# One decoder layer on one core: the first group's squares move to ScalarE and TensorE, and 1/rms comes from one reciprocal-square-root function

## The chip, the core and the metric

The kernel runs on one core of a Trainium2 chip. The core has five engines with a queue of instructions each: PE (TensorE, matmuls), DVE (VectorE), ACT (ScalarE), POOL (GpSimd) and SP (SyncE, which issues nearly all DMAs here). Each engine works through its queue in order and waits on semaphores of the others. The metric is the device time of one execution in microseconds (us).

## The reference

A layer of a hybrid decoder for 2048 prompt tokens and 8 sample tokens, model width 1024, all in float32:

```
def rms_norm(x, w):
    xf = xf * lax.rsqrt(jnp.mean(xf * xf, axis=-1, keepdims=True) + EPS)
    return (xf * w)

h = rms_norm(x, norm1_w)
q, k, v, z, xbc, dt_raw = split(h @ w_in)
a = sliding-window attention(q, k, v)              # window 128, learned sinks, relative bias
s = SSD mixer(z, xbc, dt_raw)                      # conv, scan, gate; then per group of 256 columns:
    yg = yg * lax.rsqrt(jnp.mean(yg * yg, axis=-1, keepdims=True) + EPS)
x = x + concat(a, s) @ w_out
h2 = rms_norm(x, norm2_w)
x = x + (silu(h2 @ w_gate) * (h2 @ w_up)) @ w_down
y = rms_norm(x, final_norm_w)
```

So there are four kinds of reciprocal root mean square: before the input projection, inside the SSD mixer (two per token), before the feed-forward part, and at the end.

## The kernel before, in words

Features lie on the partitions, tokens along the free axis. The 16 blocks of 128 prompt tokens are worked off in six groups: four of 384 tokens, one of 256 tokens and the 8 sample tokens (264 columns), one of 256. A float32 product is made of three fp32r matmuls (`mm3`: high times high, high times low, low times high), so each projection of one 128-column unit is 24 matmuls into one PSUM bank. A weight unit comes in two halves (`weight`, L208 to L216): SP loads the raw half, ACT makes the high part (L209), DVE the low part (L210); for a third of the units the pair is written back to HBM and read from there later (L205).

Stages are Python generators: I or X (load x, squares, 1/rms, scale), A (the dt and x/B/C projections with the convolution), K (keys, values), B (queries and gate z), P (attention), Q (SSD, then the mixer's norm), S (pair of high and low parts of the mixed heads), O (output projection), H (second norm), F (feed-forward), Z (final norm and store). The driver interleaves them by ratios written out by hand (for instance `run(("A", 0), ([("I", 0)], RI), units=UA)`); after that the tile framework's scheduler sorts the instructions of each engine by its own model of their durations, so that a small edit moves many instructions by a few places. PSUM has 8 banks, four with the tag "d" (tiles `psd`, for projections) and four with the tag "m" (tiles `psm`, for everything else).

The first group is special (`stage_x0`, kinds "I"). To let PE begin before the norm is known, x is only scaled with the norm's weight and split (L299 on ACT, L300 on DVE), and the projections run on that. What comes out of PSUM is multiplied by 1/rms afterwards (tile `r`): the dt projection in `got_dt` (L365), the x/B/C projections in `got` (L402), the keys, values, queries and z in `take`. Up to then a "d" bank stays taken. DVE squares the eight tiles of x in place (L303, eight instructions) and adds them up (L305, seven), then `rinv_b` makes 1/rms.

`rinv_b` gets the sum of squares, adds it over the partitions by one float32 matmul with a matrix of ones (`psm` from `cst`), and then has on ACT: Ln of mean plus epsilon (L695), a Copy that makes -0.5 times the mean (L697), Exp of -0.5 times the logarithm (L698), and on DVE one Newton step in three instructions (L701, L702, L703). Ln lies in another table of ACT's functions than Exp and Tanh, so an ACT_TABLE_LOAD stands ahead of the Ln and another ahead of the Exp. `rinv_b` runs for X, H and Z of every group with one sum, and for Q with two sums at once.

Tanh is used for the convolution's SiLU (L390), for z (L520) and for the feed-forward gate (L1018); Exp for softplus (L252), the SSD decays (L722, L723, L732, L749) and the softmax (L590, L592). Square, Copy and Identity never have a table load ahead of them.

Of the kernel before, what the change touches and what calls it, by code (L numbers as in the profile page):

```python
# [13 lines left out]
AF = mybir.ActivationFunctionType  # L14
ALU = mybir.AluOpType
# [14 lines left out]
DM = 1024  # L30
KT = DM // P
# [41 lines left out]
def hymba(ctx: ExitStack, tc: tile.TileContext, I: dict, O: dict, groups):  # L73
# [14 lines left out]
    def T(shape, dtype=F32, tag=None, bufs=1):  # L88
        cnt[0] += 1
        nm = f"{tag}_{cnt[0]}"  # L90
        return sb.tile(shape, dtype, tag=tag, name=nm, bufs=bufs)

    def PS(tag):
        cnt[0] += 1
        return pp.tile([P, 512], F32, tag=tag, name=f"ps{tag}_{cnt[0]}", bufs=4)
# [5 lines left out]
    V, S, G, PE, SP = nc.vector, nc.scalar, nc.gpsimd, nc.tensor, nc.sync  # L101

    def mm(o, l, r, start=True, stop=True):
        PE.matmul(o, l, r, start=start, stop=stop)  # L104
# [5 lines left out]
    ones = cst[:, C_ONE:C_ONE + P]  # L110
# [6 lines left out]
    epsc = T([P, 1], tag="epsc")  # L117
# [14 lines left out]
    bias = T([P, NH, 2 * P], tag="bias")  # L132
# [107 lines left out]
    def act_pair(home):  # L240
        return tuple(T([P, KT, NMAX], F32R, tag=home + part) for part in ("hi", "lo"))
# [27 lines left out]
    def stage_x(g):  # L269
        N, off = g["N"], g["off"]  # L270
        x = g["x"] = act_pair("a")
        xr = T([P, KT, NMAX], tag="xr")
        for h in range(2):
            ks = slice(4 * h, 4 * h + 4)
            SP.dma_start(xr[:, ks, :N], I["xT"][:, ks, off:off + N])
            yield
        sq = T([P, NMAX], tag="sq")
        yield from squares(xr, sq, N)
        yield from rinv_b(sq, N, DM)
        yield from scaled(xr, S_N1, sq, N, x, lambda m: xr[:, m, :N])  # L280


    def stage_x0(g):
        N, off = g["N"], g["off"]
        x = g["x"] = act_pair("b")
        xr = T([P, KT, NMAX], tag="xr")
        for h in range(4):
            ks = slice(2 * h, 2 * h + 2)
            SP.dma_start(xr[:, ks, :N], I["xT"][:, ks, off:off + N])
            if h == 0:  # L290
                SP.dma_start(wdr, I["wdt"])
        S.dma_start(cst, I["consts"][:, 0:C_MAIN])
        S.activation(wdt[:, :, 0:NH], wdr, AF.Copy)
        V.tensor_tensor(wdt[:, :, NH:], wdr, wdt[:, :, 0:NH].bitcast(F32), ALU.subtract)

        home = g["home"] = T([P, 2 * (FC + 1) * NMAX], tag="hc")
        r = g["r"] = T([P, NMAX], tag="m2", bufs=M2)[:, :N]
        for m in range(KT):
            S.activation(x[0][:, m, :N], xr[:, m, :N], AF.Copy, scale=col(S_N1, m))  # L299
            V.scalar_tensor_tensor(x[1][:, m, :N], xr[:, m, :N], col(S_N1, m), x[0][:, m, :N].bitcast(F32), ALU.mult, ALU.subtract)  # L300
        yield
        for m in range(KT):
            V.tensor_tensor(xr[:, m, :N], xr[:, m, :N], xr[:, m, :N], ALU.mult)  # L303
            if m:
                V.tensor_tensor(xr[:, 0, :N] if m < KT - 1 else r, xr[:, 0, :N], xr[:, m, :N], ALU.add)  # L305
            if m % 4 == 3:
                yield
        yield from rinv_b(r, N, DM)

    def take(g, ps):  # L310

# [344 lines left out]
    def stage_q(g):  # L656
        nb, N = g["nb"], g["N"]
        xbc = g["xbc"]
        for b in range(nb):
            yield from ssd(g, b)  # L660
        if g["smp"]:
            while not g.get("sdone"):
                yield
        if g["b0"] + nb == NB:
            tail_outputs(g)
        ss = []
        for q in range(2):
            s0 = T([P, NMAX], tag="tmp", bufs=6)
            s1 = T([P, NMAX], tag="tmp", bufs=6)
            S.activation(s0[:, :N], xbc[:, 2 * q, :N], AF.Square)  # L670
            S.activation(s1[:, :N], xbc[:, 2 * q + 1, :N], AF.Square)
            ss.append((s0, s1))
            yield
        for s0, s1 in ss:
            V.tensor_tensor(s0[:, :N], s0[:, :N], s1[:, :N], ALU.add)
        yield
        yield from rinv_b([s0 for s0, _ in ss], N, 256)
        for t in range(4):
            y = xbc[:, t, :N]
            V.scalar_tensor_tensor(y, y, nwc(t), ss[t // 2][0][:, :N], ALU.mult, ALU.mult)  # L680
            if t % 2:
                yield
        g["done"] = g.get("done", 0) + 1

    def rinv_b(ss, N, d):

        ss = [s[:, :N] for s in (ss if isinstance(ss, list) else [ss])]
        ps = []
        for s in ss:
            ps.append(PS("m"))  # L690
            mm(ps[-1][:, :N], ones, s)
        yield
        v = [T([P, NMAX], tag="tmp", bufs=6)[:, :N] for _ in ss]
        for s, p in zip(ss, ps):
            S.activation(s, p[:, :N], AF.Ln, bias=epsc[:, 0:1], scale=1.0 / d)  # L695
        for s, u, p in zip(ss, v, ps):
            S.activation(u, p[:, :N], AF.Copy, bias=-0.5 * EPS, scale=-0.5 / d)  # L697
            S.activation(s, s, AF.Exp, scale=-0.5)  # L698
        yield
        for s, u in zip(ss, v):  # L700
            V.tensor_tensor(u, u, s, ALU.mult)  # L701
            V.tensor_tensor(u, u, s, ALU.mult)  # L702
            V.scalar_tensor_tensor(s, u, 1.5, s, ALU.add, ALU.mult)  # L703
        yield
# [346 lines left out]
    for nb, smp in groups:  # L1051
# [6 lines left out]
    assert b0 == NB  # L1058
    n = len(gs)
    kinds = {"I": stage_x0, "X": stage_x, "A": stage_a, "K": stage_k, "B": stage_b, "P": stage_p, "Q": stage_q, "Y": stage_y,  # L1060
             "S": stage_s, "O": stage_o, "H": stage_h, "F": stage_f, "Z": stage_z}
    made = {}
# [7 lines left out]
    def run(main, *rest, units=None, drain=99):  # L1070


        rest = [e if isinstance(e, list) else [list(e[0]), e[1], 0.0] for e in rest]

        def advance(e, k):
            e[2] += k
            while e[2] >= 1 and e[0]:
                if step(*e[0][0]) == 0:
                    e[0].pop(0)
                e[2] -= 1  # L1080

        while units is None or units > 0:
            says = step(*main) if main else 0
            if says in (0, "tail"):
                break
            tick()
            for e in rest:
                advance(e, e[1])
            if units is not None:
                units -= 1  # L1090
        while any(e[0] for e in rest[:drain]):
            for e in rest[:drain]:
                e[2] = 0.0
                advance(e, 1)
            tick()
        return rest[drain:]

    def mixers(i, u):

        g = gs[i]  # L1100
        r = [([("P", i)], (g["nb"] * 20 + 1) / u), ([("Q", i)], (g["nb"] * 9 + 17 + (60 if g["smp"] else 0)) / u)]
        return r + ([([("Y", i)], 55 / (0.8 * u))] if g["smp"] else [])
# [6 lines left out]
    r = run(("A", 0), ([("X", 1)], RX1), drain=0)  # L1109
    r = run(("K", 0), *r, drain=0)  # L1110
    load_bias(bscr)
    r = run(("B", 0), *r, units=UQ, drain=0)
    r = run(("B", 0), *r, *mixers(0, U0), drain=1)
    r = run(("A", 1), *r, drain=0)
    run(("B", 1), *r, ([("S", 0)], 2), units=UB)
    run(("O", 0))
    r = run(("B", 1), ([("H", 0)], RH0), drain=0)
    run(("K", 1), *r)
    for i in range(n):
# [4 lines left out]
        elif i + 2 < n:  # L1124
            run(("F", i), *mixers(i + 1, RM), ([("X", i + 2)], RX))
            run(("F", i))
            r = run(("K", i + 2), ([("S", i + 1)], RS), ([("Z", i)], RZ), drain=0)
# [99 lines left out]
```

## Time and profile before

| what | us |
|---|---|
| median of 3 runs | 2350.46 (2349.97 to 2353.34) |
| profiled execution, its own time | 2353.68 |
| its span in the trace | 2351.9 |
| granted TensorE clock, mean over the span | 0.989 of full speed |
| DMA engines' busy share, mean rate | 75.1% on the one large queue, 252 GB/s |

The span runs from the first to the last instruction; the execution's own time is 1.8 us longer. Names in the profile are the program's tiles: `bhi,blo` and `ahi,alo` are the high and low parts of an activation pair, `w` a weight pair, `wraw` a raw weight half, `hc` the hidden tiles of the feed-forward part, `xr` the raw x, `cst` the constants with the matrix of ones, `sq`, `tmp` or `m` the tile with the sum of squares or 1/rms. `PE psd L104` is a projection's matmul (all matmuls are issued from line 104). Where a row of the timeline ends in brackets, they hold the engine's idle time before it and what ended it.

### The profile page before, as it was taken

The page shows a single profiled execution, that of the slowest core. Times are in us where ns is not written, and L with a number is a line of the kernel's source. Part 1 is how long each engine was busy: PE and PEld are TensorE (multiplying, and loading weights), DVE is VectorE, ACT ScalarE, POOL GpSimd, SP SyncE. Part 2 cuts the span into 40 slices and gives each one's busy share as a digit, 9 for nine tenths or more (in the row PEclk, how much of TensorE's full clock was granted, in tenths as well). Part 3 has the DMA queues.
Part 4 walks back from the last instruction along what each step waited for, and adds up shares of the span by engine and source line. Part 5 has one row for each costly group of instructions (what it writes and reads, how often), then busy time and mean ns, then how long its engine had stood idle before and what let it go on. Part 6 is the DMA issues. An engine that isn't in the chain of part 4 may idle for free.

```text
span 2351.9 us, 39896 instructions
## 1 busy us (share of the span) xinstructions
PE 2276.6 (97%) x14633; PEld 2224.5 (95%) x14633; DVE 1478.2 (63%) x3325; ACT 988.1 (42%) x2139; POOL 31.5 (1%) x109
## 2 busy tenths in 40 slices
PE   7995999999999999999999999999999999999997
PEld 6995999999999999999999998999999899999997
DVE  7886687866647786653566555554734567656544
ACT  5666554744444364343325333321321354434233
POOL 1000000000000000000000000000000000000000
PEclk9997999999999999999999999999999999999999
DMA  8653565666877677788777879878887987788886
GB/s 295 238 185 103 183 219 183 214 198 220 316 283 236 214 235 242 240 304 280 266 258 274 280 267 341 292 226 264 299 247 240 344 289 246 255 276 271 275 279 196
DMA packets 227230, 592.30 MB, mean 252 GB/s; under 512 B 24323, under 2 KB 64060, under 8 KB 226892
## 3 DMA queue, kind: packets, MB, share of 16 engines
q1 hardware_dynamic: 226892, 589.56, 75.1%
q8 instruction: 116, 1.90, 0.3%
q14 instruction: 78, 0.64, 0.1%
q10 hardware_dynamic: 144, 0.20, 0.0%
HBM read 479.97 MB, written 110.21 MB: 251 GB/s over the span
## 4 chain that ended last, share of the span: by engine, by line
PE 87%; DMA 6%; DVE 3%; ACT 2%; issue 1%; SPq 0%; ACTq 0%; DVEq 0%
PE psd L104 81%; PE psm L104 5%; DMA w<-wi 1%; DMA w<-wd 1%; DMA w<-wo 1%; PE psm L610 1%; DMA xr<-in_xT_dram 0%; DMA m<-sbcd 0%; DMA w<-wg 0%; DMA m<-in_sssm_dram 0%; DMA w<-wu 0%; DVE x L1045 0%; DMA big<-csd 0%; DMA out_yT_dram<-x 0%; DVE w L210 0%
## 5 line engine op out<-in xcount | busy, mean ns | idle before, releaser
L104 PE MATMUL psd<-bhi,w 128*128 128x384 f32 (+1 forms) x4448 | 1106.0, 329 | 12.6 <-DVE tmp L365 7.7
L104 PEld LDWEIGHTS psd<-bhi,w 128*128 128x128 f32 x4448 | 787.2, 189 | 20.6 <-issue 9.7
L104 PE MATMUL psd<-blo,w 128*128 128x384 f32 (+1 forms) x2224 | 727.0, 327 | 1.0 <-DVE blo L341 1.0
L209 ACT ACTIVATE w<-wraw 128x512 fp32r<-128x512 f32 (+1 forms) x543 | 324.5, 601 | 546.7 <-PE psd L104 426.4
L104 PE MATMUL psd<-hc,w 128*128 128x384 f32 (+2 forms) x3168 | 514.4, 320 | 6.2 <-DMA w<-wd 4.7
L104 PEld LDWEIGHTS psd<-hc,w 128*128 128x128 f32 x3168 | 494.4, 188 | 11.9 <-DVE sq L323 5.3
L104 PE MATMUL psd<-ahi,w 128*128 128x256 f32 (+2 forms) x2272 | 487.6, 305 | 18.4 <-DMA w<-wi 8.7
L210 DVE TENSOR_TENSOR w<-wraw,w 128x512 fp32r<-128x512 f32 (+1 forms) x543 | 353.2, 653 | 125.6 <-ACT w L209 115.8
L104 PEld LDWEIGHTS psd<-blo,w 128*128 128x128 f32 x2224 | 419.8, 189 | 2.5 <-DVE blo L341 1.3
L104 PEld LDWEIGHTS psd<-ahi,w 128*128 128x128 f32 x2272 | 377.0, 189 | 25.5 <-DMA w<-wi 7.6
L104 PE MATMUL psd<-alo,w 128*128 128x256 f32 (+2 forms) x1136 | 345.9, 305 | 0.0
L997 DVE TENSOR_TENSOR x<-psd,x 128x384 f32<-128x384 f32 (+2 forms) x336 | 169.3, 511 | 98.3 <-PE psd L104 97.6
L104 PEld LDWEIGHTS psd<-alo,w 128*128 128x128 f32 x1136 | 214.6, 189 | 1.2
L1018 ACT ACTIVATE tmp<-psd 128x384 f32<-128x384 f32 (+2 forms) x132 | 59.9, 454 | 263.0 <-PE psd L104 262.9
L1004 DVE SCALAR_TENSOR_TENSOR tmp<-tmp,psd 128x384 f32<-128x384 f32 (+2 forms) x132 | 67.0, 508 | 161.6 <-ACT tmp L1018 161.2
L1007 DVE SCALAR_TENSOR_TENSOR tmp<-psd,tmp 128x384 f32<-128x384 f32 (+2 forms) x132 | 67.7, 513 | 127.7 <-PE psd L104 127.4
L1008 ACT ACTIVATE hc<-tmp 128x384 fp32r<-128x384 f32 (+2 forms) x132 | 64.0, 485 | 142.8 <-DVE tmp L1007 142.1
L384 DVE SCALAR_TENSOR_TENSOR x<-tmp,cols,x 128x384 f32<-128x384 f32 (+1 forms) x144 | 80.6, 569 | 35.5 <-ACT x L406 26.2
L320 ACT ACTIVATE tmp<-x 128x384 f32<-128x384 f32 (+2 forms) x84 | 40.4, 487 | 102.7 <-DVE x L944 69.6
L1012 DVE TENSOR_TENSOR hc<-tmp,hc 128x384 fp32r<-128x384 f32 (+2 forms) x132 | 67.3, 510 | 16.0 <-ACT hc L1008 15.5
L323 DVE TENSOR_TENSOR sq<-sq,tmp 128x384 f32<-128x384 f32 (+2 forms) x119 | 60.5, 508 | 25.0 <-ACT tmp L320 24.1
L944 DVE TENSOR_TENSOR x<-psd,x 128x384 f32<-128x384 f32 (+2 forms) x48 | 24.7, 515 | 70.6 <-PE psd L104 70.4
(259 smaller groups left out, 1765.7 us busy)
## 6 DMA issues: line engine op xcount, KB each, us to landing
w<-wi SPq DMA_DIRECT2D x144, 512.0 KB, 5.4
w<-wu SPq DMA_DIRECT2D x133, 512.0 KB, 4.5
w<-wg SPq DMA_DIRECT2D x131, 512.0 KB, 4.6
w<-wd SPq DMA_DIRECT2D x144, 384.0 KB, 3.6
wraw<-in_wg_dram SPq DMA_DIRECT2D x133, 256.0 KB, 3.6
wraw<-in_wu_dram SPq DMA_DIRECT2D x131, 256.0 KB, 3.9
w<-wo SPq DMA_DIRECT2D x57, 512.0 KB, 4.8
wraw<-in_wd_dram SPq DMA_DIRECT2D x144, 192.0 KB, 3.6
```

What stands on the lines that cost most here:

```text
L104: PE.matmul(o, l, r, start=start, stop=stop)
L209: S.activation(hi, raw, AF.Copy)
L210: V.tensor_tensor(lo, raw, hi.bitcast(F32), ALU.subtract)
L320: S.activation(t[:, :N], x[:, m, :N], AF.Square)
L323: e.tensor_tensor(sq[:, :N], sq[:, :N], t[:, :N], ALU.add)
L384: V.scalar_tensor_tensor(acc, raw[:, j:j + NP], cwc(j, t), acc, ALU.mult, ALU.add)
L997: V.tensor_tensor(x1[:, m, :N], p[:, :N], x1[:, m, :N], ALU.add)
L1004: V.scalar_tensor_tensor(t[:, :N], t[:, :N], 1.0, pg[:, :N], ALU.add, ALU.mult)
L1007: V.scalar_tensor_tensor(t[:, :N], pu[:, :N], 0.5, t[:, :N], ALU.mult, ALU.mult)
L1008: S.activation(hh[:, 0, :N], t[:, :N], AF.Copy)
L1012: e.tensor_tensor(hl[:, 0, :N], t[:, :N], hh[:, 0, :N].bitcast(F32), ALU.subtract)
L1018: S.activation(t[:, :N], pg[:, :N], AF.Tanh, scale=0.5)
```

## The change

In `stage_x0` the squares go from DVE to ACT, and the sums from DVE to PE: each squared tile is multiplied by the matrix of ones and accumulated in one PSUM bank over eight matmuls, in place of one matmul on the finished sum. In `rinv_b`, for all groups and stages, Ln, and the Exp after it, become one function, Abs_reciprocal_sqrt; the Copy and the Newton step stay. The squares are at L304 now, the function at L697, the Copy at L699, the Newton step at L702 to L704; every line behind `rinv_b` is one higher (the feed-forward Tanh is at L1019, the first SSD Exp at L723).

```
         yield
+        ps = PS("m")
         for m in range(KT):
-            V.tensor_tensor(xr[:, m, :N], xr[:, m, :N], xr[:, m, :N], ALU.mult)
-            if m:
-                V.tensor_tensor(xr[:, 0, :N] if m < KT - 1 else r, xr[:, 0, :N], xr[:, m, :N], ALU.add)
+            S.activation(xr[:, m, :N], xr[:, m, :N], AF.Square)
+            mm(ps[:, :N], ones, xr[:, m, :N], m == 0, m == KT - 1)
             if m % 4 == 3:
                 yield
-        yield from rinv_b(r, N, DM)
+        yield from rinv_b(r, N, DM, [ps])
...
-    def rinv_b(ss, N, d):
+    def rinv_b(ss, N, d, ps=None):
...
         for s, p in zip(ss, ps):
-            S.activation(s, p[:, :N], AF.Ln, bias=epsc[:, 0:1], scale=1.0 / d)
+            S.activation(s, p[:, :N], AF.Abs_reciprocal_sqrt, bias=epsc[:, 0:1], scale=1.0 / d)
         for s, u, p in zip(ss, v, ps):
             S.activation(u, p[:, :N], AF.Copy, bias=-0.5 * EPS, scale=-0.5 / d)
-            S.activation(s, s, AF.Exp, scale=-0.5)
```

The order of the instructions changes with it. PE's queue at the start, before: the place where the first group's dt projection (`psd_128`) meets the first x/B/C projections (`psd_172`, `psd_214`); the one matmul for the sum of squares comes 63 rows further on.

```order
L104 MATMUL psm_118<-m_20_119,rb_115 8x384
L104 MATMUL psd_128<-blo_82,wdt_73 16x384
L104 MATMUL psd_128<-bhi_81,wdt_73 16x384
L104 MATMUL psd_128<-blo_82,wdt_73 16x384
L104 MATMUL psd_128<-bhi_81,wdt_73 16x384
L104 MATMUL psd_172<-bhi_81,w_25_161 128x384
L104 MATMUL psd_172<-blo_82,w_25_161 128x384
```

PE's queue at the same place now, where `psm_145` is the sum of squares and `xr_83` the squared x:

```order
L104 MATMUL psm_118<-m_20_119,rb_115 8x384
L104 MATMUL psm_145<-xr_83,cst_63 128x384 x2
L104 MATMUL psd_128<-bhi_81,wdt_73 16x384
L104 MATMUL psd_128<-blo_82,wdt_73 16x384
L104 MATMUL psd_128<-bhi_81,wdt_73 16x384
L104 MATMUL psm_145<-xr_83,cst_63 128x384
L104 MATMUL psd_128<-blo_82,wdt_73 16x384
L104 MATMUL psm_145<-xr_83,cst_63 128x384
L104 MATMUL psd_128<-bhi_81,wdt_73 16x384
```

All eight sums now stand among the dt matmuls and the first four matmuls of the first x/B/C projection, ahead of its other twenty.

ACT's queue at the same time now (before, all eight L299 stood ahead of the first L209, and there was no L304):

```order
L299 ACTIVATE bhi_81<-xr_83,cols_68 128x384 x2
L304 ACTIVATE xr_83<-xr_83 128x384 x2
L299 ACTIVATE bhi_81<-xr_83,cols_68 128x384 x2
L304 ACTIVATE xr_83<-xr_83 128x384 x2
L299 ACTIVATE bhi_81<-xr_83,cols_68 128x384 x2
L209 ACTIVATE w_26_163<-wraw_164 128x512
L304 ACTIVATE xr_83<-xr_83 128x384 x2
L209 ACTIVATE w_29_169<-wraw_170 128x512
L209 ACTIVATE w_33_205<-wraw_206 128x512
L304 ACTIVATE xr_83<-xr_83 128x384
L209 ACTIVATE w_35_210<-wraw_211 128x512
L304 ACTIVATE xr_83<-xr_83 128x384
```

The squares stand between the parts of x and the first weight halves.

ACT's queue at the first group's mixer norm (stage Q), before: two sums, `psm_1817` and `psm_1819`; L638 and L550 belong to the attention of the group's second and third block, L404 and L406 take the second group's x/B/C projection out of its bank (`psd_1837`).

```order
L695 ACT_TABLE_LOAD
L695 ACTIVATE tmp_1740<-psm_1817,epsc_64 128x384
L697 ACTIVATE tmp_1821<-psm_1817 128x384
L638 ACTIVATE m_328_1804<-psm_1795 64x512
L698 ACT_TABLE_LOAD
L698 ACTIVATE tmp_1740<-tmp_1740 128x384
L695 ACT_TABLE_LOAD
L695 ACTIVATE tmp_1744<-psm_1819,epsc_64 128x384
L697 ACTIVATE tmp_1822<-psm_1819 128x384
L404 ACTIVATE tmp_1862<-psd_1837 128x384
L406 ACTIVATE x_235_1304<-psd_1837,cols_68 128x384
L390 ACT_TABLE_LOAD
```

The same place now; `psd_1833` is the same projection.

```order
L697 ACT_TABLE_LOAD
L697 ACTIVATE tmp_1738<-psm_1815,epsc_64 128x384
L699 ACTIVATE tmp_1819<-psm_1815 128x384
L638 ACTIVATE m_328_1802<-psm_1793 64x512
L697 ACTIVATE tmp_1742<-psm_1817,epsc_64 128x384
L699 ACTIVATE tmp_1820<-psm_1817 128x384
L404 ACTIVATE tmp_1858<-psd_1833 128x384
L406 ACTIVATE x_235_1302<-psd_1833,cols_68 128x384
L390 ACT_TABLE_LOAD
```

Between the first sum and L406 two table loads and one Exp are gone. Over the whole program the table loads go from 53 to 48: one at the start, 24 ahead of the new function, and 23 ahead of the next Tanh or Exp after it (ten at L1019, five at L520, three each at L252 and L390, one each at L590 and L723).

More of the change, by code (lines that the diff above doesn't have):

```diff
@@ L683, in stage_q @@
         g["done"] = g.get("done", 0) + 1
-    def rinv_b(ss, N, d):
+    def rinv_b(ss, N, d, ps=None):
         ss = [s[:, :N] for s in (ss if isinstance(ss, list) else [ss])]
[L688 to L692, printed above, removed]
+        if ps is None:
+            ps = []
+            for s in ss:
+                ps.append(PS("m"))
+                mm(ps[-1][:, :N], ones, s)
+            yield
         v = [T([P, NMAX], tag="tmp", bufs=6)[:, :N] for _ in ss]
         for s, p in zip(ss, ps):
-            S.activation(s, p[:, :N], AF.Ln, bias=epsc[:, 0:1], scale=1.0 / d)
+            S.activation(s, p[:, :N], AF.Abs_reciprocal_sqrt, bias=epsc[:, 0:1], scale=1.0 / d)
         for s, u, p in zip(ss, v, ps):
             S.activation(u, p[:, :N], AF.Copy, bias=-0.5 * EPS, scale=-0.5 / d)
-            S.activation(s, s, AF.Exp, scale=-0.5)
         yield
```

## The prediction

> **What bounds the kernel now.** I read the page first. PE is busy for nearly the whole span, so only two things can shorten the kernel: less work for PE, or fewer of the moments in which PE stands still or runs at the lower clock.
>
> ```profile
> PE 2276.6 (97%) x14633; PEld 2224.5 (95%) x14633; DVE 1478.2 (63%) x3325; ACT 988.1 (42%) x2139; POOL 31.5 (1%) x109
> ```
>
> Next, PE's waits, longest first; the columns are total us, times, longest.
>
> ```profile
> PE psm L610 <- ACT big L605: 16.9, 1, 16.9
> PE psd L104 <- DVE tmp L365: 7.7, 1, 7.7
> ...
> PE psd L104 <- ACT x L406: 5.8, 3, 4.4
> ...
> PE psd L104 <- DVE tmp L1004: 0.2, 1, 0.2
> ```
>
> The first two are single events, and one event makes up 4.4 of the third row's 5.8 us; all lie in the first 220 us. The stretches of time say what lies around them: PE's busy time, the granted clock (PEclk) and the DMA share.
>
> ```profile
> 7.24:10.65 3.41, 2.77 (x8) 0.52 (x7) 3.18 (x8) 3.25 (x7) 0.00 (x0) 1.00 1.09 396
> ...
> 27.50:35.20 7.70, 0.01 (x1) 0.03 (x1) 3.06 (x6) 3.69 (x6) 0.00 (x0) 0.74 1.05 375
> 35.20:41.40 6.20, 6.20 (x19) 6.20 (x20) 6.20 (x13) 2.53 (x4) 0.95 (x4) 0.50 0.62 253
> 202.50:219.50 17.00, 0.06 (x2) 0.01 (x1) 14.55 (x45) 9.17 (x30) 0.00 (x0) 0.58 0.42 141
> 232.50:2339.20 2106.70, 2084.72 (x13560) 2047.85 (x13559) 1282.81 (x2850) 841.66 (x1825) 15.58 (x72) 1.00 0.77 258
> ```
>
> From 232.5 us to 2339.2 us PE is busy for 2084.7 of 2106.7 us at full clock. Whatever the change does to ACT or DVE there is hidden, unless it opens a new wait. So I look at three sites: the start, the first group's mixer norm (around 190 us) and the tail.
>
> **Site 1, the start.** The timeline, PE, DVE and ACT together, from the dt projection to the end of the first long wait:
>
> ```profile
> 10.09 1.44 PE L104 MATMUL psm<-m,rb 33*8 33x384 f32 x2 [0.63 <-DMA m<-in_consts_dram]
> ...
> 13.36 0.52 PE L104 MATMUL psd<-blo,wdt 128*16 128x384 f32 x1
> 13.68 0.52 PE L104 MATMUL psd<-bhi,wdt 128*16 128x384 f32 x1
> ...
> 14.38 0.34 PE L104 MATMUL psd<-blo,wdt 128*16 128x384 f32 x1
> 14.56 0.34 PE L104 MATMUL psd<-bhi,wdt 128*16 128x384 f32 x1
> ...
> 23.38 0.55 DVE L305 TENSOR_TENSOR m<-xr 128x384 f32<-128x384 f32 x1
> ...
> 25.48 1.28 ACT L695 ACT_TABLE_LOAD   x1
> ...
> 25.84 0.34 PE L104 MATMUL psd<-blo,w 128*128 128x384 f32 x1
> ...
> 26.36 0.34 PE L104 MATMUL psd<-blo,w 128*128 128x384 f32 x1
> ...
> 26.54 0.81 PE L104 MATMUL psm<-m,cst 128*128 128x384 f32 x2
> 26.89 0.63 PE L104 MATMUL psd<-bhi,w 128*128 128x384 f32 x1
> ...
> 32.17 0.52 ACT L698 ACTIVATE m<-m 128x384 f32<-128x384 f32 x1
> ...
> 34.51 0.55 DVE L365 TENSOR_TENSOR tmp<-psd,m 16x384 f32<-16x384 f32 x1
> ...
> 35.20 0.66 PE L104 MATMUL psd<-bhi,w 128*128 128x384 f32 x1 [7.69 <-DVE tmp L365]
> ```
>
> DVE finishes the sum of squares at 23.9 us, PE sums it over the partitions at 26.5, and behind the logarithm, a weight conversion, a wait for the next x, a second table load, the exponential and the Newton step r is there at 34.5. By 27.5 PE has filled all four "d" banks (dt and three projections) and waits 7.7 us. Then it works to 41.4 at half clock, the 19 matmuls of the second stretch.
>
> What would it be without this? One matmul at full clock takes 0.173 us (three from 25.84 to 26.36), so the 19 are worth 3.3 us: before stands at 41.4 where a PE at full clock that starts the fourth projection at 41.4 - 3.3 = **38.1 us** would stand. The question is when it starts it after the change.
>
> ACT's rows at the start:
>
> ```profile
> 7.31 3.42 ACT L299 ACTIVATE bhi<-xr,cols 128x384 fp32r<-128x384 f32 x6 [1.19 <-DMA xr<-in_xT_dram]
> 10.64 2.37 ACT L209 ACTIVATE w<-wraw 128x512 fp32r<-128x512 f32 x4
> 17.51 0.63 ACT L209 ACTIVATE w<-wraw 128x512 fp32r<-128x512 f32 x1 [4.50 <-DMA wraw<-in_wi_dram]
> ```
>
> and what a Square and the two kinds of table load cost there (the group's columns: busy us, mean ns):
>
> ```profile
> L320 ACT ACTIVATE tmp<-x 128x384 f32<-128x384 f32 (+2 forms) x84 | 40.4, 487 | 102.7 <-DVE x L944 69.6
> L695 ACT ACT_TABLE_LOAD x26 | 33.4, 1283 | 0.5
> L698 ACT ACT_TABLE_LOAD x25 | 32.1, 1283 | 0.4
> ```
>
> ACT had 4.5 us without work before 17.5; eight squares at 0.49 us are 3.9 us. I walk the new order from 7.31: six L299 at 0.57 (3.4), four L209 at 0.59 (2.4), the squares 3.9: ACT is through the last square and the fourth weight half at 17.0 us, just before the fifth raw half lands. The squares cost ACT nothing that counts. DVE loses fifteen instructions, none of which is awaited any more.
>
> PE pays. The sum matmul at 26.54 pushes the end of the next matmul from 26.54 + 0.34 to 27.52: 0.64 us for a float32 product in its two passes. At half clock I take twice that, 1.28: the same two-pass form takes 1.44 us at 10.09. In the new order PE does the dt products as before and the table product to about 11.4, then two sums at half clock to 14.0, where in the trace of before the matmuls go from 0.32 us apart (13.36, 13.68) to 0.18 (14.38, 14.56). Then come six sums (3.8), eight dt matmuls (1.4) and four of the first projection (0.7): 19.9 us. The last square (17.0) is not waited for. The other 68 matmuls of the three projections (11.8) end at **31.7 us**.
>
> Is r there by then? The fifth weight half is some 0.7 us later than before, since its DMA stands behind one more on SP, so ACT reaches the new table load at 18.8 and is done with it at 20.1, with the function and the Copy at 21.2; three Newton instructions, one weight half between them and L365 at about 0.55 each: 24.3. That is 7 us ahead of need; the wait goes and with it the slow stretch. Gain: 38.1 - 31.7 = 6.4; I take **6.0**. The lower bound is 0: in 27.5 to 35.2 the DMA share was 1.05, and these transfers must now run while PE consumes weights. The upper bound is 8.7, if nothing delayed PE beyond the last square (17.0 + 0.6 + 11.8 = 29.4).
>
> The Trainium skill ("TensorE: Matmul & The Clock Gate", "Part 1: The HAM clock gate") says that the array starts at half clock, is released after a busy window of 3.4 us, and falls back after an idle one. The trace agrees: PEclk is 0.50 behind the 7.7 us wait.
>
> **Site 2, the first group's mixer norm.** ACT's timeline:
>
> ```profile
> 187.96 0.58 ACT L695 ACTIVATE tmp<-psm,epsc 128x384 f32<-128x384 f32 x1 [0.80 <-PE psm L104]
> ...
> 193.91 0.68 ACT L406 ACTIVATE x<-psd,cols 128x384 f32<-128x384 f32 x1
> 194.61 1.28 ACT L390 ACT_TABLE_LOAD   x1
> ...
> 198.78 0.53 ACT L698 ACTIVATE tmp<-tmp 128x384 f32<-128x384 f32 x1
> 199.33 0.42 ACT L550 ACTIVATE m<-kT 64x256 fp32r<-64x256 f32 x1
> ```
>
> The 4.4 us wait for L406 is this queue: between the first logarithm and L406 stand two table loads and an Exp that the new order lacks, 2 x 1.28 + 0.53 = 3.1 us. A second Exp (0.53) stood ahead of the last L550, with which the group's third attention block begins. That block ends in the 16.9 us wait, a chain of ACT and DVE steps that simply starts earlier when its L550 does. So 3.6 us at most come off by removal alone, and PE reaches the sums some 0.6 us sooner in the new order, 4.2 in all. Against it, a second L404, L406 pair and a weight half now stand ahead of the L550s (about 1.7). DVE is busy for 14.6 of the 17.0 us, and if it sets the pace nothing is gained. Between 0 and 4.2 I take **3.0**, since DVE's own start of this stretch waits for the same queue.
>
> **Site 3, the tail.** The last rows of ACT's timeline:
>
> ```profile
> 2341.83 0.38 ACT L697 ACTIVATE tmp<-psm 128x256 f32<-128x256 f32 x1
> 2342.22 1.28 ACT L698 ACT_TABLE_LOAD   x1
> 2343.51 0.42 ACT L698 ACTIVATE sq<-sq 128x256 f32<-128x256 f32 x1
> ```
>
> Nothing covers these. The load and the Exp go: **1.7 us** (2342.22 to 2343.93).
>
> The new function has no row. It reads the operands that L695 reads, so I give it L695's 0.58; between 0.49 (Square) and twice that the sum changes by 0.1 to 0.6 us at each site, and no gain is excluded: Copy takes 0.38 on 256 columns.
>
> **Everything else.** In `rinv_b` ACT does one instruction less per sum, but every next Tanh or Exp now brings the table back: 23 loads of 1.28 us, at places where none stood. What covers them:
>
> ```profile
> L1018 ACT ACTIVATE tmp<-psd 128x384 f32<-128x384 f32 (+2 forms) x132 | 59.9, 454 | 263.0 <-PE psd L104 262.9
> ```
>
> ACT sat idle for 263 us before these Tanhs, waiting for PE. A bank is needed again only three projections later, 3 x 24 x 0.173 = 12.5 us. PE's wait for what follows the Tanh (L1004) was 0.2 us in the whole run. I cost the loads at nothing; with that cover gone they cost 23 x 1.28 = 29.5.
>
> The Trainium skill ("ScalarE: Activation LUTs", "Table sets: the hidden batching unit") says that Ln and Exp lie together in one set, so that Ln followed by Exp takes one load. The trace differs: 26 loads at L695 and 25 at L698. By that rule the tail would gain the Exp alone, 0.4, and site 2 one load less.
>
> **The sum.** 6.0 + 3.0 + 1.7 = 10.7 us: the profiled execution's 2353.7 would become 2343.0. The median of the runs shown, 2350.5, is 3.2 us below that execution, and becomes 2339.8, which I predict. A measurement of this kernel can tell about 0.2% from no change, 4.7 us.
>
> **The rivals.**
> - *All as said* (gain 8 to 14): 2336 to 2343. Chance 0.55.
> - *The clock rises late.* In the new order PE has more short waits before 14 us. If the clock rises one step of 3.4 us later, PE loses 1.7: 2341.5. For it: between 7.24 and 10.65 us PE was busy for 2.77 of 3.41 us even before. Against: the sums are long and fill the time behind. 0.13.
> - *The start is given back to DMA.* PE no longer pauses, so the big transfers of the first 60 us (the next x, the bias table) meet weight loads that PE needs, and the projections behind the fourth wait for `wraw`. Sites 2 and 3 stay: 4.7 us, 2345.8, up to 2347.5 if site 2 gives half. For it: DMA share 1.05 at 375 GB/s. Against: PE's list of waits has no long DMA wait. 0.22.
> - *No effect:* PE waits as long for squares and sums as it did for r, and DVE sets site 2; 1.7 us remain, 2348.8. Against it: ACT's 4.5 idle us. 0.04.
> - *Slower: the reloads are exposed.* Each Tanh behind a norm comes 1.28 us later, and the gate frees its bank too late. From the ninth load that PE feels, the gain is eaten (10.7 / 1.28 = 8.3); with all 23, 18.8 us are lost, 2369.3. For it: 23 new places on the way from PSUM. Against: 0.2 us of waiting at L1004. 0.06.
>
> **How the numbers follow.** The first two cases lie over 4.7 us faster, and half of the third: 0.55 + 0.13 + 0.11 = 0.79. Within 0.2% are the other half of the third and the fourth, 0.15; slower 0.06. The range, 2335 to 2347.5, goes from the upper bounds (8.7 + 4.2 + 1.7 = 14.6, with 0.9 for the spread of runs) to the worse end of the third case; it leaves out the last two.
>
> **What would show it.** Site 1 right: no wait of PE for L365, the fourth projection's first matmul near 32 us, no half clock around 35 us. Site 2 right: the wait for L406 under 2 us, the L610 after the long wait 8 to 9 us earlier than 219.5. Site 3 right: one table load behind the last matmul. The prediction is wrong if PE waits for `wraw` or `w` in the first 60 us, if the clock stays at half beyond 17 us, or if waits for L1005 or other readers of a Tanh appear among PE's longest.

## The result, and the profile after

The changed kernel takes 2336.9 us (median of four runs, 2335.6 to 2339.7); the kernel before, beside it, 2351.9 (2350.0 to 2354.3). The ratio is 0.9932 with a 95% interval of 0.992 to 0.9944: faster by 15 us. The forecast was 2339.8 in a range of 2335.0 to 2347.5. So 15.0 us were gained where 10.7 were forecast; the times lie closer than that, 2.9 us apart, because the kernel before ran 1.4 us slower beside the changed one than in the runs from which the forecast started. The profiled execution of after has a span of 2337.9 us against 2351.9, so 14.0 less.

Engine busy time on the page, and PE's longest waits (columns as before):

```profile
PE 2277.3 (97%) x14647; PEld 2225.7 (95%) x14647; DVE 1471.7 (63%) x3310; ACT 973.1 (42%) x2112; POOL 29.4 (1%) x109
```

```profile
PE psm L610 <- ACT big L605: 17.0, 1, 17.0
PE psd L104 <- DMA w<-wi: 12.6, 9, 2.9
PE psd L104 <- DVE wdt L294: 6.6, 1, 6.6
PE psd L104 <- DMA w<-wd: 6.2, 6, 1.5
PE psd L104 <- ACT bhi L927: 2.0, 1, 2.0
```

The 7.7 us wait for L365 is gone, and no wait for a reader of a Tanh (L1005) came in. The 17 us wait for L605 has its old length; what counts there is when it ends.

**The start.** Timeline rows of after, from the last squares to the fourth projection's first matmul:

```profile
14.58 0.51 ACT L304 ACTIVATE xr<-xr 128x384 f32<-128x384 f32 x1
...
17.48 1.28 ACT L697 ACT_TABLE_LOAD   x1
...
19.28 1.45 PE L104 MATMUL psm<-xr,cst 128*128 128x384 f32 x4
...
20.77 0.58 ACT L697 ACTIVATE m<-psm,epsc 128x384 f32<-128x384 f32 x1 [2.00 <-PE psm L104]
...
24.02 0.55 DVE L365 TENSOR_TENSOR tmp<-psd,m 16x384 f32<-16x384 f32 x1
...
32.18 0.51 PE L104 MATMUL psd<-bhi,w 128*128 128x384 f32 x2
```

The table load is over before PE's sum is, the function takes the 0.58 us of the logarithm, and r is there at 24.0, eight us ahead of need. The fourth projection begins with the second matmul of the last row, at 32.4, and the stretch of time behind it (PE's busy time, then the clock) shows full speed:

```profile
32.30:37.50 5.20, 5.20 (x32) 4.92 (x31) 4.06 (x9) 2.61 (x4) 0.31 (x2) 1.00 1.04 399
```

**The first group's mixer norm.** ACT's rows of before that the prediction did not show, then those of after. L507 takes a query projection out of its bank; the first L590 of each fence is the softmax of the second attention block, the last one that of the third:

```profile
166.40 0.49 ACT L507 ACTIVATE qT<-psd 128x384 f32<-128x384 f32 x1 [1.65 <-PE psd L104]
...
167.32 0.51 ACT L590 ACTIVATE big<-big,sm 128x256 f32<-128x256 f32 x1
...
213.90 0.51 ACT L590 ACTIVATE big<-big,sm 128x256 f32<-128x256 f32 x1
```

```profile
156.63 0.51 ACT L590 ACTIVATE big<-big,sm 128x256 f32<-128x256 f32 x1 [1.40 <-DVE sm L584]
...
160.69 0.47 ACT L507 ACTIVATE qT<-psd 128x384 f32<-128x384 f32 x1
...
177.22 0.58 ACT L697 ACTIVATE tmp<-psm,epsc 128x384 f32<-128x384 f32 x1 [2.21 <-PE psm L104]
...
185.44 1.72 ACT L550 ACTIVATE m<-kT 64x256 fp32r<-64x256 f32 x4
...
202.59 0.51 ACT L590 ACTIVATE big<-big,sm 128x256 f32<-128x256 f32 x1 [1.80 <-DVE sm L584]
```

PE's transposes behind the long wait follow at the same distance as before:

```profile
208.19 2.53 PE L610 MATMUL psm<-cst,big 128*128 128x128 f32 x8 [17.03 <-ACT big L605]
```

L590 and L610 start 11.3 us earlier than before, of which the start explains 5.8.

**The tail.** One table load is left, and it lies beside the last matmul:

```profile
2327.90 1.28 ACT L697 ACT_TABLE_LOAD   x1
...
2328.49 0.67 PE L104 MATMUL psm<-sq,cst 128*128 128x256 f32 x2 [1.58 <-DVE sq L323]
2329.20 0.47 ACT L697 ACTIVATE sq<-psm,epsc 128x256 f32<-128x256 f32 x1
```

**Where the 14 us are.** Projections have the same matmuls in every kernel of this case, so the n-th can be compared with the n-th (those of the small dt projections are not counted). This table, worked out from the traces, has the change of each stretch's length against the kernel before, in us (one execution each; minus is shorter). The stretches: to the 385th projection matmul (94 us before), then to the 913th (251 us), to the 1701st (408 us), to the last, and from its start to the end of the span.

| kernel | start | mixer norm | next norm | the long middle | tail | sum |
|---|---|---|---|---|---|---|
| after | -5.8 | -5.6 | -2.6 | +1.7 | -1.7 | -14.0 |
| e1_squares | -5.4 | -2.5 | 0.0 | +2.6 | 0.0 | -5.3 |
| e2_function | -5.5 | +1.6 | -2.6 | -0.4 | -1.7 | -8.6 |
| e3_act_dve | -11.4 | -2.7 | -2.6 | -3.9 | -1.7 | -22.3 |
| e4_q_lnexp | -6.2 | -0.6 | -2.6 | +3.9 | -1.7 | -7.2 |
| e5_h_z_lnexp | -9.0 | -5.5 | 0.0 | 0.0 | 0.0 | -14.4 |
| e6_reloads | -5.9 | -5.5 | -0.9 | +9.4 | -1.7 | -4.6 |
| e7_warm | -5.9 | -2.5 | -2.6 | +4.4 | -1.7 | -8.4 |
| e8_warm_q_lnexp | -6.3 | +1.0 | -2.6 | -3.1 | -1.7 | -12.7 |
| e9_halves | -7.9 | -8.0 | -2.6 | -1.0 | -1.7 | -21.2 |
| e10_warm16 | -5.8 | -5.6 | -2.6 | -2.7 | -1.7 | -18.4 |
| e11_halves_warm16 | -8.3 | -6.8 | -2.6 | +4.2 | -1.7 | -15.2 |

The middle is some 1930 us of feed-forward and projections that the change hardly touches; there single executions differ by weight waits and clock steps of 1 to 4 us (e4's +3.9 holds one wait of 3.7 us for a weight). So a site is read from its own column, and a total from the medians.

### The profile page after: what moved, and what is told of

It is laid out like the page before. It is cut to its first block, busy times and chain, and to the rows that moved or that the text cites. A ratio compares the mean times of both kernels' runs of the same rounds, so it can differ in the third digit from the quotient of the medians.

```text
span 2337.9 us, 39913 instructions
## 1 busy us (share of the span) xinstructions
PE 2277.3 (97%) x14647; PEld 2225.7 (95%) x14647; DVE 1471.7 (63%) x3310; ACT 973.1 (42%) x2112; POOL 29.4 (1%) x109
## 4 chain that ended last, share of the span: by engine, by line
PE 90%; DMA 5%; DVE 3%; ACT 1%; issue 0%; SPq 0%; DVEq 0%; ACTq 0%
PE psd L104 82%; PE psm L104 6%; DMA w<-wi 2%; DMA w<-wd 1%; DMA out_yT_dram<-x 1%; DVE x L1046 1%; DMA m<-sbcd 1%; PE psm L610 1%; DMA m<-in_sssm_dram 0%; PE psm L731 0%; DMA w<-wu 0%; DMA w<-wo 0%; DMA w<-wg 0%; DVE w L210 0%; DVE big L570 0%
## 5 line engine op out<-in xcount | busy, mean ns | idle before, releaser
L209 ACT ACTIVATE w<-wraw 128x512 fp32r<-128x512 f32 (+1 forms) x543 | 324.3, 601 | 536.2 <-PE psd L104 420.4
L104 PEld LDWEIGHTS psd<-ahi,w 128*128 128x128 f32 x2272 | 378.0, 190 | 22.0 <-DMA w<-wi 10.3
L1005 DVE SCALAR_TENSOR_TENSOR tmp<-tmp,psd 128x384 f32<-128x384 f32 (+2 forms) x132 | 66.9, 507 | 173.9 <-ACT tmp L1019 173.6
L1019 ACT ACTIVATE tmp<-psd 128x384 f32<-128x384 f32 (+2 forms) x132 | 60.1, 455 | 248.0 <-PE psd L104 247.9
```

Of the source, the lines that this page charges most:

```text
L209: S.activation(hi, raw, AF.Copy)
L1005: V.scalar_tensor_tensor(t[:, :N], t[:, :N], 1.0, pg[:, :N], ALU.add, ALU.mult)
L1019: S.activation(t[:, :N], pg[:, :N], AF.Tanh, scale=0.5)
```

## Experiments

**One part alone.** Only the squares and their sums, with Ln and Exp kept:

```
-            S.activation(s, p[:, :N], AF.Abs_reciprocal_sqrt, bias=epsc[:, 0:1], scale=1.0 / d)
+            S.activation(s, p[:, :N], AF.Ln, bias=epsc[:, 0:1], scale=1.0 / d)
...
+            S.activation(s, s, AF.Exp, scale=-0.5)
```

> Only the first group's squares on ScalarE and their sum on TensorE; every norm keeps Ln and Exp. Theory (three sites that add up, each with its own cause): the start gains all of its 5.7 us, since r, even with two table loads and the Exp, takes some 8 us from its sum as before, so about 29 us, still ahead of the fourth projection at 32.4; the first group's mixer norm, the norm behind it and the tail gain nothing. Total 5.7 us, ratio 0.9976. Rival (the start needs both parts): r is later than 32.4 us, PE waits for L365 again, and the start gains 3 us or less, total ratio 0.9987 or more.

Measured: ratio 0.998 (0.9971 to 0.9989), 5.1 us by the medians. ACT's and DVE's rows at the start:

```profile
20.48 0.58 ACT L697 ACTIVATE m<-psm,epsc 128x384 f32<-128x384 f32 x1 [1.41 <-PE psm L104]
21.46 1.28 ACT L700 ACT_TABLE_LOAD   x1
22.76 0.53 ACT L700 ACTIVATE m<-m 128x384 f32<-128x384 f32 x1
```

```profile
25.62 0.55 DVE L365 TENSOR_TENSOR tmp<-psd,m 16x384 f32<-16x384 f32 x1
```

L365 is only 1.6 us later than with the new function, and still ahead of need. The start gains all it can, the next norm and the tail nothing, as the theory had it; it did not have the 2.5 us at the mixer norm, which come without the new function.

Only the new function, with the first group's squares on DVE (shown against the kernel after):

```
...
-            S.activation(xr[:, m, :N], xr[:, m, :N], AF.Square)
-            mm(ps[:, :N], ones, xr[:, m, :N], m == 0, m == KT - 1)
+            V.tensor_tensor(xr[:, m, :N], xr[:, m, :N], xr[:, m, :N], ALU.mult)
+            if m:
+                V.tensor_tensor(xr[:, 0, :N] if m < KT - 1 else r, xr[:, 0, :N], xr[:, m, :N], ALU.add)
...
-        yield from rinv_b(r, N, DM, [ps])
+        yield from rinv_b(r, N, DM)
```

> Only the new function in every norm; the first group's squares and their sum stay on VectorE. Theory: PE's wait for L365 at the start shrinks from 7.7 to about 3.7 us (the table load, the Exp and the queue between go), which gives 4 us, and 7 if the clock stays up over the shorter wait; the first group's mixer norm gives 5.6, the norm behind it 2.6, the tail 1.7. Total 14 to 17 us, as much as the whole change or more, because PE is spared the 5.7 us of sums. Rival (the later sites gain because the start was moved, not because of the function): the mixer norm gives 3 us or less and the norm behind it nothing; total 6 to 9 us.

Measured: ratio 0.9956 (0.9944 to 0.9969), 10.8 us. PE's waits have

```profile
PE psd L104 <- DVE tmp L365: 3.9, 1, 3.9
```

and the start gained 5.5 us, between the 4 and the 7 that were expected; the next norm and the tail went as said. But the mixer norm lost 1.6 us where 5.6 of gain were expected, so the total lies between the theory's 14 to 17 us and the rival's 6 to 9. PE's timeline, and a stretch of time behind it, show part of it:

```profile
160.57 0.45 PE L104 MATMUL psd<-ahi,w 128*128 128x384 f32 x1 [2.06 <-ACT qT L507]
```

```profile
160.98:164.39 3.41, 3.41 (x13) 3.41 (x12) 3.41 (x10) 0.06 (x1) 0.00 (x0) 0.50 0.02 4
```

A wait of 2.1 us for a Q eviction (L507), and a step of half clock behind it (0.50). At that site the parts do not add up, -2.5 and +1.6 to -5.6, and my theory of independent sites falls there. At the start they do not either: the squares alone gain 5.4 us, the function alone 5.5, and both together 5.8. The function alone leaves PE a wait of 3.9 us but no added sums; with the squares moved the wait is gone and PE has the sums to do.

**Undo the function at single norms.** Mixer norms alone back on Ln and Exp:

```
-            S.activation(s, p[:, :N], AF.Abs_reciprocal_sqrt, bias=epsc[:, 0:1], scale=1.0 / d)
+            S.activation(s, p[:, :N], AF.Ln if d == 256 else AF.Abs_reciprocal_sqrt, bias=epsc[:, 0:1], scale=1.0 / d)
...
+            if d == 256:
+                S.activation(s, s, AF.Exp, scale=-0.5)
```

> The whole change, but the mixer norms (both halves of 256 channels, in every group) keep Ln and Exp. Theory (at the first group's mixer norm the two table loads and the Exp on ScalarE's queue are what the gain comes from): its 5.6 us are given back, start, next norm and tail stay as with the whole change: 8.4 us below the kernel before, ratio 0.9964. Rival (the earlier sums, or the shift of the start against the DMAs, give that site its gain): 2 us or less are given back, 12 us or more stay, ratio 0.995 or less.

Measured: ratio 0.9955 (0.9942 to 0.9968), 10.4 us, and the mixer norm gives back 5.0 of 5.6; the total alone could not tell theory from rival, since 0.9964 and 0.995 both lie in the interval. PE's order is the whole change's but for a handful of rows, so ACT's rows can be set beside those of after:

```profile
176.83 0.58 ACT L697 ACTIVATE tmp<-psm,epsc 128x384 f32<-128x384 f32 x1 [2.21 <-PE psm L104]
...
188.63 1.72 ACT L550 ACTIVATE m<-kT 64x256 fp32r<-64x256 f32 x4
...
205.79 0.51 ACT L590 ACTIVATE big<-big,sm 128x256 f32<-128x256 f32 x1 [2.48 <-DVE sm L584]
```

From the first function to the end of the last L550 it is 13.5 us, in after 9.9 (177.22 to 187.16). The difference, 3.6, is what the function takes off ACT's queue, the very sum of the prediction (two loads and two Exps). The other 1.4 us came behind the wait, where the clock stayed at half until 226.2 us, in after only until 213.9 and for one more step: 0.3 of them ahead of the next projection, which starts at 220.41 us, and 1.1 in it.

Ln and Exp back in the norms behind the mixer and at the end (both calls; `rinv_b` then makes Ln and Exp again):

```
-        yield from rinv_b(sq, N, DM)
+        yield from rinv_b(sq, N, DM, lnexp=True)
```

> The whole change, but the norms behind the mixer and the final norms keep Ln and Exp; the first group's squares, the first norm and the mixer norms stay as changed. Theory (each of these norms has its own gain, from the table load and the Exp that go): 2.6 us are given back between 240 and 390 us, where PE waits for L341 again, and 1.7 us in the tail; the rest stays, so the time is 4.3 us over that of the whole change, ratio 0.995. Rival (the gain between 240 and 390 us comes from the earlier start of that stretch, not from its function): only the 1.7 us of the tail are given back, ratio 0.994.

Measured: ratio 0.9947 (0.9935 to 0.9959), in which the theory's 0.995 and the rival's 0.994 both lie. The table decides: it shows the two sites given back whole: 2.6 us and 1.7 us; PE waits again for the low part of the feed-forward's input, as it did before:

```profile
PE psd L104 <- DVE blo L341: 1.0, 1, 1.0
```

and the tail has its second load:

```profile
2327.79 1.28 ACT L703 ACT_TABLE_LOAD   x1
2329.09 0.42 ACT L703 ACTIVATE sq<-sq 128x256 f32<-128x256 f32 x1
```

In all traces with the function in this norm but one the stretch of the next norm is 154.65 us, without it 157.23 (the exception is e6 below). The theory held.

**Spare PE the sums.** The squares stay on ACT; DVE adds them up and PE makes one sum:

```
-        ps = PS("m")
...
-            mm(ps[:, :N], ones, xr[:, m, :N], m == 0, m == KT - 1)
+            if m:
+                V.tensor_tensor(xr[:, 0, :N] if m < KT - 1 else r, xr[:, 0, :N], xr[:, m, :N], ALU.add)
...
-        yield from rinv_b(r, N, DM, [ps])
+        yield from rinv_b(r, N, DM)
```

> The whole change, but the eight squares that ScalarE makes are added up by VectorE in seven additions, and PE makes one sum over the partitions instead of eight. Theory (PE's sums lie on the path and cost 5.0 of their 5.65 us beyond the one that must stay): the fourth projection starts near 27.4 us, r is there by about 24 to 26, and the time is 5 us below that of the whole change: 19 us below the kernel before, ratio 0.992 against it. Rival (the sums only fill time in which PE would wait for weights or for r anyway): the time is that of the whole change within 1.5 us.

Measured: ratio 0.9916 (0.9904 to 0.9928), 20.4 us by the medians, the lowest ratio here; its interval only just overlaps the whole change's.

```profile
19.45 0.81 PE L104 MATMUL psm<-m,cst 128*128 128x384 f32 x2
```

```profile
26.77 0.41 PE L104 MATMUL psd<-bhi,w 128*128 128x384 f32 x1 [0.27 <-DVE tmp L365]
```

The fourth projection starts at 26.8 instead of 32.4, and r is just in time (PE waits 0.27 us for L365). Some of that is the clock, which rose at 10.2 us in this execution. A cleaner measure is the kernel with two sums below, where the clock rose at 14.5 us, against e4 with eight, where it rose at 14.6: there that projection starts at 27.8 and 32.0, so six sums cost 4.2 us, and by that the seven that the change adds cost some 4.9 on PE's path (an estimate, 7/6 of 4.2), close to the theory's 5.0. The mixer norm, however, gains only 2.7 here:

```profile
176.45 0.58 ACT L697 ACTIVATE tmp<-psm,epsc 128x384 f32<-128x384 f32 x1 [0.80 <-PE psm L104]
...
182.84 1.73 ACT L550 ACTIVATE m<-kT 64x256 fp32r<-64x256 f32 x4
...
199.80 0.52 ACT L590 ACTIVATE big<-big,sm 128x256 f32<-128x256 f32 x1
```

The first function is 11.5 us earlier than before, just what the start gave; in after it came 10.7 earlier with a start worth 5.8. The order that the scheduler made differs: here, as before, the second block's softmax stands behind the Q eviction. With the sums added in two halves of four (DVE six additions, PE two sums) that order comes back:

```
-            mm(ps[:, :N], ones, xr[:, m, :N], m == 0, m == KT - 1)
+            if m % 4:
+                V.tensor_tensor(xr[:, m - m % 4, :N], xr[:, m - m % 4, :N], xr[:, m, :N], ALU.add)
+            if m % 4 == 3 or m == KT - 1:
+                mm(ps[:, :N], ones, xr[:, m - m % 4, :N], m < 4, m == KT - 1)
```

> The whole change, but VectorE adds up the first group's squares in two halves (six additions) and PE sums two tiles over the partitions instead of eight. ScalarE's order around the first group's mixer norm is then the whole change's again (the second block's softmax ahead of a projection's eviction, both evictions ahead of the last L550s), which it was not with one sum. Theory (there the gain of the whole change, 5.6 us, was made of the order, which brought the first sum 5.0 us earlier against the start, and of the 3.6 us that the function takes off ScalarE's queue; with VectorE's single sum the site gained 2.8): the start gains 10 to 11 us, the mixer norm 5 to 6, the next norm 2.6, the tail 1.7: 20 us, 2 to 3 us below the kernel with one sum, ratio 0.991. Rival (the site's gain hangs on where clock steps and weight loads fall, not on this order): it gains 3 us or less, and the time is that of the kernel with one sum or above it.

Measured: ratio 0.9924 (0.991 to 0.9937).

```profile
173.75 0.58 ACT L700 ACTIVATE tmp<-psm,epsc 128x384 f32<-128x384 f32 x1 [1.35 <-PE psm L104]
...
182.62 1.73 ACT L553 ACTIVATE m<-kT 64x256 fp32r<-64x256 f32 x4
...
199.32 0.51 ACT L593 ACTIVATE big<-big,sm 128x256 f32<-128x256 f32 x1 [1.80 <-DVE sm L587]
```

With the order, the first function is 14.2 us earlier than before, 6.3 more than the start's 7.9, and the site gains 8.0, more than the 5 to 6 that were expected: against the rival, the gain came with the order. The total did not follow. Up to 51 us the start gave 10.3, as expected, but by 94 us it gave only 7.9, mostly since PE waited for a weight's low part,

```profile
PE psd L104 <- DVE w L210: 2.2, 3, 1.1
```

and the time is that of the kernel with one sum within the intervals, as the rival had it.

**The rival of the exposed reloads.** One more function of the other table set ahead of every feed-forward Tanh:

```
+            S.activation(t[:, 0:1], pg[:, 0:1], AF.Abs_reciprocal_sqrt)
             S.activation(t[:, :N], pg[:, :N], AF.Tanh, scale=0.5)
```

> The whole change with one more function of the other table set on one column of the gate's PSUM tile ahead of every feed-forward Tanh, 132 times; its result is overwritten by the Tanh, so nothing is left out. Behind the matmuls of a gate stands now a small function, a table load of 1.28 us and only then the Tanh, about 1.6 us later than before, 132 times instead of at a few; some 340 us of table loads are added. Theory (12.5 us pass before the gate's bank is needed again): hidden but for places where PE waits for a Tanh's product at a stage's end; the time stays within 4 us of the whole change, ratio 0.993 to 0.995. Rival (reloads are felt by PE): from 132 times 1.28 us, 169 us, ratio 1.06, or a good part of it.

Measured: ratio 0.9987 (0.9976 to 0.9998), over the whole change by 13 us in the ratio and 10 in the medians. The groups of the page (busy us, mean ns; the added function is at L1019 here, the Tanh at L1020):

```profile
L1020 ACT ACT_TABLE_LOAD x128 | 164.2, 1283 | 2.3
L1019 ACT ACT_TABLE_LOAD x122 | 156.5, 1283 | 4.2 <-PE psd L104 2.1
```

and new among PE's waits:

```profile
PE psd L104 <- ACT hc L1009: 2.4, 2, 2.2
PE psd L104 <- DVE tmp L1008: 2.1, 2, 1.6
PE psd L104 <- DVE tmp L1005: 2.0, 1, 2.0
```

Neither expectation is met: 10 to 13 us, not 4 and not 169. Some 240 more loads than in after, with the added small functions, are felt with 0.05 us each on the mean, at the few places where PE waits for the end of a gate. The change's own reloads are 23, ten of them at this Tanh, with none of these waits: nothing, within what can be measured.

**What the half clock costs behind the 17 us wait.** Unread matmuls, ahead of L610's transposes of the third block, keep PE busy through the wait:

```
             ps = PS("m")
+            if g["b0"] == 0 and b == 2 and kv == 0:
+                for _ in range(24):
+                    mm(ps[:, 0:384], ones, cst[:, 0:384])
```

> The whole change, with 24 matmuls that nobody reads (128x384, float32, 0.64 us each at full clock, 15.4 us) ahead of the transposes of L610 for which PE waits 17.0 us in the first group; they write the bank that the transposes then overwrite. Theory (part of what that site cost before and costs still is the half clock behind the wait: 5.7 us and another 3.4 us of busy time): the clock stays up through the wait, PE's wait shrinks to 1 or 2 us without the transposes starting later, and up to 4.6 us are gained, ratio 0.991 to 0.992. Rival (what follows the wait is paced by ScalarE and VectorE, not by PE's clock): under 1 us is gained, or some is lost because the transposes start later.

> The same 24 matmuls in the kernel in which only the mixer norms keep Ln and Exp. In that kernel without them the site lost 5.0 us against the whole change: PE was idle for 1.9 us more, and after the long wait the clock stayed at half for 14.8 us instead of 5.7 and 3.4. Theory (the table loads and the Exp themselves are worth some 2 us of waiting, and the rest was the clock's): with the clock held up in both, the two kernels differ by about 2 us. Rival (all 5.0 us are the queue of ScalarE): they still differ by 5 us.

Measured: ratios 0.9938 (0.9925 to 0.9951) and 0.9964 (0.9951 to 0.9977). Twenty-four were too many: they began only when a bank was free, ran at half clock until 199.5 us, and pushed the transposes to 212.4 us.

```profile
194.11 18.40 PE L104 MATMUL psm<-cst 128*128 128x384 f32 x48 [3.04 <-DVE sm L570]
```

By itself the first run settles nothing. The pair tells something: from the 385th to the 913th matmul the two differ by 3.6 us (153.8 and 157.3), not by 2 and not by 5.0. That fits the 3.6 us of the queue and the 1.4 of the clock that e4 showed, from one execution of each. With 16 matmuls in place of 24 in the whole change:

> The whole change with 16 instead of 24 unread matmuls ahead of L610's transposes; with 24 the transposes started at 212.4 instead of 208.2 us. 16 of them, from 194.1 us, partly at half clock, end near 207.1 us, ahead of the 207.7 us at which ScalarE starts L605. Theory (the half clock behind the wait costs what PE's own work there shows, some 4 us): 3 to 4 us are gained. Rival (between the transposes and the next projection ScalarE and VectorE set the pace; with 24 matmuls that stretch took 7.5 instead of 8.7 us): 1.2 us there, and 1.7 more at most where the clock then stays up in the projection behind it.

Measured: ratio 0.9934 (0.9922 to 0.9946), the whole change's, and the mixer norm's column is the whole change's too (-5.6). The stretch behind the wait, first of this kernel and then of after (PE's busy time, its matmuls, and the clock, which comes after POOL):

```profile
208.10:217.00 8.90, 6.08 (x17) 2.62 (x17) 5.22 (x10) 4.97 (x14) 0.00 (x0) 1.00 0.01 2
```

```profile
208.10:217.00 8.90, 6.76 (x17) 3.64 (x17) 5.28 (x10) 5.03 (x14) 0.00 (x0) 0.67 0.00 0
```

The clock stayed up, and the next projection still began at 216.90 us in both. Between the transposes and that projection ACT and DVE set the pace, so the half clock there, up to 213.9 us, costs nothing; even the rival's 1.2 us was too much. With the halves:

> The two edits together: squares added up in two halves, and 16 unread matmuls ahead of L610. If the sites are independent of each other, the gains add up: the start and the mixer norm as in the first, and 1 to 3 us from the clock as in the second, 21 to 23 us below the kernel before, ratio 0.9905. Rival: the clock's steps of 3.4 us fall elsewhere and the second gain is gone.

Measured: ratio 0.9922 (0.9909 to 0.9936), no gain over the halves alone. That is the rival's outcome, but not for its reason alone: the 16 matmuls had no gain over the whole change either, so there was none to add.

## Why the prediction was right, and where not

The time was in the range and the way was right; the size was 10.7 us forecast and 14.0 in the trace. Two errors went the same way, 2.6 us too little at site 2 and 2.6 us at a norm that the sum did not hold; 0.2 us at the start and 1.7 in the long middle went the other way.

**Site 1** was right, and so was its mechanism. Forecast 6.0, measured 5.7 (from 42 to 72 us every projection is 5.74 earlier). The last square came at 15.1 instead of 17.0 and was not waited for, L365 ended at 24.6 (forecast 24.3, though its terms add up to about 24.0), the fourth projection at 32.4 (31.7). The clock can explain the 0.7 us: it rose at 15.9 in this execution, not at 14.1 as before, which at half speed is 0.9, a small part of the rival of the late clock. That the squares alone gain as much here (e1), and the function alone too (e2), the prediction did not separate; it gave the site to both parts together. The rival in which the gain goes back to DMA did not come: no weight is waited for in the first 60 us. (The upper end of that rival, 2347.5, is 2347.3 by its own terms.)

**Site 2** was right in direction and too small, 3.0 against 5.6, outside its upper bound of 4.2. The terms, from the rows above, net of the start's 5.8:

- "PE reaches the sums some 0.6 us sooner in the new order": **4.9 us** sooner (187.96 to 177.22 is 10.7). This is the step that failed. I looked at the last stretch of the order, from the squares to the sum, and not at what comes ahead of it: the second block's softmax (L590 at 156.63) now stands before a Q eviction (L507 at 160.69) for which ACT used to wait first (166.40, with the softmax at 167.32), and the mixer's squares come earlier with it.
- Removal of two loads and two Exps, 3.6: measured 3.6 (e4).
- The L404, L406 pair and the weight half ahead of the L550s, 1.7 against: 13.5 in e4 less 11.8 before (187.96 to 199.75) is 1.7.
- From the last L550 to the softmax it now takes 15.4 us instead of 14.2, so 1.3 against: the stretch of which the prediction warned, without a price, that DVE may set its pace. Why it became longer was not followed up.

In sum 4.9 + 3.6 - 1.7 - 1.3 = 5.5. That the first term is not the mixer norm's own function is shown by e4, which has Ln and Exp there and the same 4.9 (176.83, with a start worth 6.2), and by e3, which has the function and 0.2. It goes with the softmax's place: with the softmax ahead of that eviction it is 3.0 in e1, which has the function nowhere, 4.9 in after, e4 and e5, and 6.3 in e9; with the softmax behind it, it is 0.2 in e3 and -2.7 in e2. No run moves the softmax alone, so that it is the cause is likely and not shown. The forecast did not count on it: the site's gain of the whole change rests at least as much on the order that the scheduler happened to make as on the function, and that part was luck.

**Site 3**: 1.7 forecast, 1.7 measured, and undone by e5.

**What was missed**: 2.6 us at the norm behind the first group's mixer. The prediction looked there only for losses. Before, PE waited 1.0 us for L341 at the first feed-forward matmuls, a row of the same list of waits that I did not follow up; behind that wait lay the same load and Exp, and e5 gives the 2.6 us back. The list of waits accounts for 1.2 of them (this row and 0.2 us for L209); the rest does not stand in it as waiting.

**The costs put at nothing** were right: the 23 reloads (by e6 a reload at a feed-forward Tanh costs some 0.05 us on the mean, 1.2 us for all 23 if each cost that). The stretch in the middle gave 1.7 us back in the profiled execution, but over kernels without added reloads it went from -3.9 to +4.4, so no effect of the change can be read from it.

As to the signs: no wait for L365, no half clock around 35 us, L406 at 1.0 us, one load at the tail all came; L610 came 11.3 us earlier, not 8 to 9.

The Trainium skill ("ScalarE: Activation LUTs", "Table sets: the hidden batching unit") would have given the tail the Exp alone, 0.4 us, since it puts Ln and Exp in one set. The measurement decides against it: 1.7 us, and the load comes back with e5.

## What to carry to other kernels

A chain on ACT is worth shortening where another engine waits at its end, and that is read from the list of waits down to the waits of one us: the missed norm, worth 2.6 us, showed there as a row of 1.0. When work is taken off one engine's path, price it on the engine that gets it: squares moved to ACT made nothing wait here, sums moved to PE cost some 4.9 us, and with the additions left on DVE the start gained 11.4 us in place of 5.8, part of it by an early rise of the clock. Where a scheduler sorts the instructions, follow what moved ahead of the edited site too, and do not expect the parts of an edit to add up there.

## What the runs showed of the hardware

- The moment of the first rise of the clock differs between executions of the same instructions. Seven kernels share the start of after; in six the clock rose between 14.6 and 15.9 us, in one (e5) at 9.4. Over the same 6.5 us PE does 12 matmuls in after and 25 in e5:

```profile
9.40:15.90 6.50, 6.50 (x12) 2.71 (x11) 5.15 (x11) 5.69 (x13) 0.00 (x0) 1.00 0.69 250
```

```profile
9.40:15.90 6.50, 6.50 (x25) 3.55 (x26) 4.95 (x11) 5.49 (x12) 0.00 (x0) 1.00 0.67 235
```

  (The clock column of these two rows has no record yet for the part ahead of the rise.) That makes 3.1 us in the start column of the table, -9.0 against -5.8, where the two kernels do not differ. The Trainium skill ("TensorE: Matmul & The Clock Gate", "Part 1: The HAM clock gate") has the clock released after a busy window of about 3.4 us and the window free-running, so that the same kernel ramps at different times. These runs agree that the moment varies. They do not show that one busy window is enough, or needed: counted back from the rise in after, the step from 9.11 to 12.52 us was busy throughout (3.41 us) without a release, and in e5 the step that ended with the rise was busy for 2.75 of 3.42 us.
- Abs_reciprocal_sqrt from PSUM takes what Ln takes: 0.58 us on 384 columns, 0.47 on 256.
- A half clock cost nothing where PE waited for others between its matmuls: 0.67 against 1.00 over 8.9 us, and the next projection began at the same 216.90 us. In e4, at half clock throughout, the same stretch took 9.0 us in place of 8.7.
